# Narrower and longer weight tiles for one q projection, and four gelus written one product later

## The chip, the cores and the metric

The kernel runs on one core of a Trainium2 chip. Time is device microseconds (us) of one execution; a lower number is better. Besides the timed runs there is one profiled execution, whose trace gives start and duration of every instruction on the five engines: PE (TensorE matmuls, with PEld for its weight loads), DVE (VectorE), ACT (ScalarE), POOL (GpSimd) and SP (SyncE, here only the issuing of DMAs).

## The reference

A trunk of two layers over 1024 tokens of width 1024, all in float32. Layer A is a gated MLP whose spatial mixing is per chunk of 128 tokens; layer B is sliding-window attention with sinks; both are wrapped in RMS norms.

```python
# layer A (gmlp_mixer), h = rms_norm(x)
u, v, z = split(h @ w_in, 3)                # 1024 x 2048 each
u = gelu(u)
v = layer_norm(gelu(v), ln_g, ln_b)
s = einsum(causal W_s per chunk and group, v) + b_s
y = (u * s * silu(z)) @ w_out
h1 = x + rms_norm(y)
# shared keys and values
k, v = rms_norm(h1) @ w_k, rms_norm(h1) @ w_v
# layer B (swa_mixer), h = rms_norm(h1)
q, z = split(h @ w_in, 2)                   # 1024 x 1024 each
o = softmax(q k + alibi, with sinks, window 128) v
out = h1 + rms_norm((o * silu(z)) @ w_out)
```

## The kernel before, in words

**Precision.** Each float32 product is made of three fast matmuls: both operands are split into a high part (`hi`, rounded) and a low part (`lo`, what rounding left), and `mm3` (lines 169 to 171) adds hi·hi, hi·lo and lo·hi into one PSUM bank. A split is one ACT instruction for `hi` and one DVE instruction for `lo`: `split` (lines 105 and 106), or `split_scaled` (lines 109 and 110), which multiplies by a gain of one value per partition on the way. The gain belongs to a contraction row block k, so a weight tile that holds several k is split by one `split_scaled` per k.

**Layer A, v.** `v_layer` computes gelu(v) with seven block products instead of eight (a Strassen scheme) for each column half Q. The products come in the order m = 1, 2, 5, 6, 7, 4, 3, each in two steps u = 0, 1 of 24 matmuls. Products 1, 6, 7 and 4 accumulate one after the other in the same four PSUM banks (`vb`); after 1, 6 and 7 ACT copies the running sums out (`copy`, line 209) while the sums stay in the banks, so the next product may write a bank only when its copy is done. Products 2, and 5 with 3, go to four other banks (`vc`). A finished block t gets `done`: a gelu on ACT with the per-token scale `rx` (line 391) and `bn_stats` on DVE (line 392), and the four blocks are stored by one DMA that ACT issues (line 388). For the first block `a1` and for `e67`, the gelus of Q = 0 are written later than their sums, by the table `late` (line 468): `a1` after the matmuls of step (7, 0), `e67` after those of (3, 0). `rx[0]` comes from four token loads, squares on ACT (line 183, tile `junk_x`), a DVE step (line 178) and a power on POOL (line 179). The generator `side` writes these squares, one block of 128 tokens per step from the fifth step on: x_stats(0) in steps (5, 0) to (6, 1), x_stats(1) in steps (7, 0) to (4, 1).

**Layer A, u, z and output projection.** `uz_layer` and `out_layer` follow in the same manner; the first three weight tiles of layer B are loaded towards the end of `out_layer`.

**Layer B.** Tokens go in two halves of 512. For half 0 come q (`q_phase`), the shared k and v (`kv_phase`), then z; half 1 follows, filled in between attention units. `Weights` holds the list of all weight tiles in order, 512 KB each; `wnext` hands out a tile, has the next one split (two `whi`/`wlo` buffers) and the third next loaded (three `raw` buffers, issued by SP). `qz_four` takes four tiles (kq = 0 to 3) for four output blocks m to m+3: a tile holds four m by two k (the 128 x 128 blocks), gives 24 matmuls, and all four banks are complete only in the last of the four tiles. Then `evac` empties each bank: two ACT copies of 64 partitions (line 976, tiles `q_hi` and `q_lo`) and two DVE instructions (line 980). For q of half 0 the first four m use the PSUM banks of tag `mm`, the other four those of tag `s`. `kv_phase` opens four `mm` banks at its start (two `pk`, two `pv`). Beside q of half 0 runs `chain_a(1)`, which finishes layer A's second token half (line 760 on DVE, squares on ACT); beside kv runs `norm_h1(1)`, which transposes on PE into `s` banks (line 776).

**Order.** The order on each engine is not that of the source. The framework's planner walks through the program with its own estimates of durations; whenever an engine is free it is given, of the instructions that the planner then holds to be ready, the one written first. On the chip each engine keeps the order so fixed and waits where an input is late.

Of the kernel before, what the change touches and what calls it, by code (L numbers as in the profile page):

```python
# [19 lines left out]
KT = D // P  # L20
# [7 lines left out]
G_PRE, G_LNG, G_LNB, G_KV, G_BPRE = 0, 8, 24, 40, 48  # L28
# [6 lines left out]
def step(*gens):  # L35
    for g in gens:
        next(g, None)
# [13 lines left out]
def tile_yoco(  # L51
# [29 lines left out]
    def bank(tag, name):  # L81
        return psum.tile([P, 512], F32, tag=tag, name=name)
# [12 lines left out]
    def raw_tile(name):  # L95
        return wpool.tile([P, 1024], F32, tag="raw", name=f"raw_{name}", bufs=3)

    def wload(src, name):
        raw = raw_tile(name)
        dst = raw if len(src.shape) == 2 else raw.rearrange("p (m c) -> p m c", m=4)  # L100
        nc.sync.dma_start(out=dst, in_=src)
        return raw

    def split(hi, lo, src):
        nc.scalar.activation(hi, src, AF.Copy)  # L105
        nc.vector.tensor_tensor(lo, src, hi.bitcast(F32), ALU.subtract)  # L106

    def split_scaled(hi, lo, src, g):
        nc.scalar.activation(hi, src, AF.Copy, scale=g)  # L109
        nc.vector.scalar_tensor_tensor(lo, src, g, hi.bitcast(F32), ALU.mult, ALU.subtract)  # L110

    class Weights:


        def __init__(self):
            self.order = []
            q, z = ([(wqz[i, m:m + 4, :, kq * 256:kq * 256 + 256].rearrange("m p c -> p m c"), f"q{kq}")
                     for m in range(0, 8, 4) for kq in range(4)] for i in range(2))
            kv = [(wkv[kp], f"kv{kp}") for kp in range(4)]
            self.order += q + kv + z + kv + q + z  # L120
            self.order += [(wo_b[gd, cp], "") for gd in range(2) for cp in range(4)]
            self.raw, self.done, self.at = [], [], 0

# [6 lines left out]
        def split(self, i):  # L130
            while len(self.done) <= min(i, len(self.order) - 1):
                n = len(self.done)
                self.load(n)
                raw, kind = self.raw[n], self.order[n][1]
                hi = wpool.tile([P, 1024], F32R, tag="whi", name=f"whi{n}")
                lo = wpool.tile([P, 1024], F32R, tag="wlo", name=f"wlo{n}")
                halves = [slice(kk * 512, kk * 512 + 512) for kk in range(2)]
                if kind[:1] == "q":
                    hv, lv, rv = (t.rearrange("p (m k c) -> p m k c", m=4, k=2) for t in (hi, lo, raw))
                    for k in range(2):  # L140
                        split_scaled(hv[:, :, k], lv[:, :, k], rv[:, :, k], gain(G_BPRE, 2 * int(kind[1:]) + k))
                elif kind[:2] == "kv":
                    for kk, cs in enumerate(halves):
                        split_scaled(hi[:, cs], lo[:, cs], raw[:, cs], gain(G_KV, 2 * int(kind[2:]) + kk))
                else:
                    split(hi, lo, raw)
                self.done.append((hi, lo))
# [10 lines left out]
    def gain(c, k):  # L158
        return gn[:, c + k:c + k + 1]
# [3 lines left out]
    def wnext():  # L163
        w = weights.get()
        weights.ahead()
        return w

    def mm3(out, a_hi, a_lo, b_hi, b_lo, start, stop):
        nc.tensor.matmul(out, lhsT=a_hi, rhs=b_hi, start=start, stop=False, skip_group_check=True)  # L169
        nc.tensor.matmul(out, lhsT=a_hi, rhs=b_lo, start=False, stop=False, skip_group_check=True)  # L170
        nc.tensor.matmul(out, lhsT=a_lo, rhs=b_hi, start=False, stop=stop, skip_group_check=True)  # L171
# [126 lines left out]
    def v_layer(ahead):  # L298
# [140 lines left out]
        a1, e6, e67 = [], None, []  # L439
        for n, (Q, m, u) in enumerate(steps):  # L440
            if u == 0:
                if m == 1:
                    bank_b = [bank("mm", f"vb{Q}_{t}") for t in range(4)]
                elif m in (2, 5):
                    bank_c = [bank("s", f"vc{Q}{m}_{t}") for t in range(4)]
            ps = bank_b if m in (1, 6, 7, 4) else bank_c
            first = m in (1, 2, 5)
            hi, lo = ready.pop(n)
            for kk in range(2):
                k = 2 * u + kk  # L450
                cs = slice(kk * 512, kk * 512 + 512)
                for t in range(4):
                    ts_ = slice(t * P, (t + 1) * P)
                    mm3(ps[t], T[m][0][:, k, ts_], T[m][1][:, k, ts_], hi[:, cs], lo[:, cs],
                        first and k == 0, k == HT - 1)
            if n >= 2:
                prep(n + 2)
            if n >= len(steps) - 3:
                step(ahead)
            if n == 0:  # L460
                xload(xa[:, 1], 0, 1, 0, 2)
            elif n == 1:
                prep(3)
                xload(xa[:, 1], 0, 1, 2, 2)
            elif n >= 4:
                step(side)

            late = {(7, 0): (a1, 0), (3, 0): (e67, 1)}.get((m, u)) if Q == 0 else None
            if late:
                for t in range(4):  # L470
                    done(late[0][t], late[0][t], late[1], late[1], t, Q)
                store(slots[late[1]], late[1], late[1], Q)
            if u == 0:
                continue
            for t in range(4):
                if m == 1:
                    a1.append(slots[0][:, t])
                    copy(a1[t], ps[t])
                elif m == 2:
                    add(a1[t], a1[t], ps[t], ALU.add)  # L480
                    if Q:
                        done(a1[t], a1[t], 0, 0, t, Q)
                elif m == 6:
                    if t == 0:
                        e6 = big.tile([P, 4, TH], F32, tag="P1_3", name=f"ve6_{Q}")
                    copy(e6[:, t], ps[t])
                elif m == 7:
                    e67.append(slots[1][:, t])
                    copy(e67[t], ps[t])
                    add(e67[t], e67[t], bank_c[t], ALU.add)  # L490
                    if Q:
                        done(e67[t], e67[t], 1, 1, t, Q)
                elif m == 4:
                    c = slots[Q][:, t]
                    done(c, ps[t], 1, 0, t, Q)
                elif m == 3:
                    add(e6[:, t], e6[:, t], ps[t], ALU.add)
                    done(e6[:, t], e6[:, t], 0, 1, t, Q)
            block = {3: (e6, 0, 1), 4: (slots[Q], 1, 0)}.get(m)
            if Q and m in (2, 7):  # L500
                block = (slots[0], 0, 0) if m == 2 else (slots[1], 1, 1)
            if block:
                store(*block, Q)
            if m == 3:
                a1, e67 = [], []
            if Q == 1 and m == 2:
                broadcast_rstd(vp)
# [437 lines left out]
    kh = [bp.tile([P, 2, S], F32R, name=f"kh{i}") for i in range(2)]  # L945
# [11 lines left out]

    def qz_four(h, which, m, n, evac):

        tag = "s" if (h, which, m) in ((0, 0, 4), (0, 1, 0)) else "mm"  # L960
        ps = [bank(tag, f"qz{h}_{which}_{m + i}") for i in range(4)]
        for kq in range(4):
            hi, lo = (t.rearrange("p (m k c) -> p m k c", m=4, k=2) for t in wnext())
            for i in range(4):
                for kk in range(2):
                    k = 2 * kq + kk
                    mm3(ps[i], hi[:, i, kk], lo[:, i, kk], n[0][:, k], n[1][:, k], k == 0, k == KT - 1)
                if kq == 3:
                    evac(m + i, ps[i])
                yield  # L970

    def q_phase(h, n, q):
        def evac(m, ps):
            for par in range(2):
                rw = half[par]
                nc.scalar.activation(q[par][rw, m], ps[rw], AF.Copy, scale=qsc[rw, m // 4:m // 4 + 1])
            for par in range(2):
                rw, ot = half[par], half[1 - par]
                g = qsc[rw, m // 4:m // 4 + 1]
                nc.vector.scalar_tensor_tensor(q[par][ot, m], ps[rw], g, q[par][rw, m].bitcast(F32),  # L980
                                               ALU.mult, ALU.subtract)

        for m in range(0, 8, 4):
            yield from qz_four(h, 0, m, n, evac)

    def z_phase(h, n, z, m0, m1):
        def evac(m, ps):
# [314 lines left out]
```

## Time and profile before

| what | value |
|---|---|
| median of three runs | 1050.24 us (1049.72 to 1050.43) |
| the profiled execution's own time | 1051.19 us |
| its span, first to last instruction | 1049.4 us |
| mean granted TensorE clock | 0.998 |
| PE busy | 1038.2 us, 99% of the span |
| DVE, ACT, POOL busy | 731.8, 579.8, 199.5 us |

The span is what the trace covers; the profiled execution's own time holds 1.8 us more, and the median of the unprofiled runs lies 0.95 us below it. A row of the timeline gives start, duration, engine, line, operation, output and inputs with shapes, how often, and in brackets how long the engine sat idle before and who ended that wait. Matmuls overlap: a 128x512 matmul is shown with 0.39 us, but such matmuls start 0.227 us apart.

### The profile page before, as it was taken

How to read it: one execution, taken by the hardware profiler on the slowest of the kernel's cores; microseconds unless marked ns; L12 is line 12 of the kernel's file. 1: busy time of each engine (PE TensorE's matmuls, PEld its weight loads, DVE VectorE, ACT ScalarE, POOL GpSimd, SP SyncE). 2: the span in 40 equal slices, each digit the busy share in tenths (PEclk: the TensorE clock that was granted, in tenths of full speed). 3: DMA queues.
4: the chain of work that ended last, by engine and by line, in shares of the span. 5: the costliest groups of instructions: out<-in, count | busy, mean ns of one | idle time of the engine just before them, and what ended most of it. 6: DMA issues, size and time to landing. Idle time of an engine off the chain costs nothing.

```text
span 1049.4 us, 13678 instructions
## 1 busy us (share of the span) xinstructions
PE 1038.2 (99%) x4994; PEld 854.8 (81%) x4994; DVE 731.8 (70%) x1244; ACT 579.8 (55%) x998; POOL 199.5 (19%) x153
## 2 busy tenths in 40 slices
PE   9999999999999999999999999999999999999997
PEld 7878888888888888888888888888888777877776
DVE  6987566867768668677696587765247786667763
ACT  6584344565565465655444465654466665786631
POOL 0500003253442552530200000100001111011120
PEclk9999999999999999999999999999999999999999
DMA  8878242324333333247998543532322121211363
GB/s 309 271 262 292 101 171 94 116 101 146 126 117 120 123 134 116 101 140 265 320 354 282 195 167 93 200 102 82 99 81 66 56 81 61 81 61 62 121 220 121
DMA packets 80899, 157.56 MB, mean 150 GB/s; under 512 B 5824, under 2 KB 32704, under 8 KB 80832
## 3 DMA queue, kind: packets, MB, share of 16 engines
q1 hardware_dynamic: 76320, 148.01, 41.4%
q10 hardware_dynamic: 4512, 8.68, 2.3%
q8 instruction: 39, 0.64, 0.3%
q14 instruction: 28, 0.23, 0.1%
HBM read 125.21 MB, written 31.46 MB: 149 GB/s over the span
## 4 chain that ended last, share of the span: by engine, by line
PE 93%; DVE 3%; DMA 2%; ACT 1%; issue 0%; SPq 0%; DVEq 0%; POOLq 0%; ACTq 0%
PE qz L169 6%; PE ob L169 6%; PE ub L169 6%; PE qz L171 6%; PE ub L170 6%; PE ub L171 6%; PE ob L171 6%; PE ob L170 6%; PE qz L170 6%; PE s L1058 3%; PE uc L170 3%; PE uc L169 3%; PE uc L171 3%; PE sp L621 3%; PE oc L169 2%; PE oc L171 2%
## 5 line engine op out<-in xcount | busy, mean ns | idle before, releaser
L110 DVE SCALAR_TENSOR_TENSOR wlo<-raw_w,gn,whi 128x512 fp32r<-128x512 f32 x80 | 58.5, 757 | 62.2 <-ACT whi L109 62.0
L169 PE MATMUL qz<-n_hi,whi 128*128 128x512 f32 x256 | 100.9, 394 | 0.0
L171 PE MATMUL qz<-n_hi,wlo 128*128 128x512 f32 x256 | 99.8, 390 | 1.1 <-DVE wlo L110 1.1
L170 PE MATMUL qz<-n_lo,whi 128*128 128x512 f32 x256 | 99.9, 390 | 0.0
L109 ACT ACTIVATE whi<-raw_w,gn 128x512 fp32r<-128x512 f32 x80 | 54.8, 716 | 56.8 <-PE qz L170 36.6
L1073 ACT ACTIVATE pr<-pr,mx 128x129 f32<-128x129 f32 x128 | 50.1, 393 | 39.8 <-DVE mx L1069 39.8
L169 PEld LDWEIGHTS qz<-n_hi,whi 128*128 128x128 f32 x256 | 48.1, 188 | 15.8 <-issue 5.7
L105 ACT ACTIVATE uzhilo_g<-f 128x1024 fp32r<-128x1024 f32 x31 | 32.9, 1060 | 49.2 <-PE uc L171 43.3
L171 PEld LDWEIGHTS qz<-n_hi,wlo 128*128 128x128 f32 x256 | 48.0, 188 | 11.8 <-DVE wlo L110 1.5
L170 PEld LDWEIGHTS qz<-n_lo,whi 128*128 128x128 f32 x256 | 48.1, 188 | 9.3
L106 DVE TENSOR_TENSOR uzhilo_g<-f,uzhilo_g 128x1024 fp32r<-128x1024 f32 x31 | 38.6, 1245 | 19.9 <-ACT uzhilo_g L105 19.9
L209 ACT ACTIVATE uz_slots<-ub 128x512 f32<-128x512 f32 x48 | 28.3, 590 | 42.4 <-PE ub L171 39.2
L169 PE MATMUL ub<-T,whi_g 128*128 128x512 f32 x128 | 50.7, 396 | 0.0
L169 PE MATMUL ub<-T,uzhilo_g 128*128 128x512 f32 x128 | 50.5, 395 | 0.0
L171 PE MATMUL ub<-T,wlo_g 128*128 128x512 f32 x128 | 49.9, 390 | 0.0
L171 PE MATMUL ub<-T,uzhilo_g 128*128 128x512 f32 x128 | 49.9, 390 | 0.0
L170 PE MATMUL ub<-T,uzhilo_g 128*128 128x512 f32 x128 | 49.9, 390 | 0.0
L170 PE MATMUL ub<-T,whi_g 128*128 128x512 f32 x128 | 49.8, 389 | 0.0
L169 PE MATMUL uc<-T,uzhilo_g 128*128 128x512 f32 x124 | 48.9, 395 | 0.0
L170 PE MATMUL uc<-T,uzhilo_g 128*128 128x512 f32 x124 | 48.3, 389 | 0.0
L171 PE MATMUL uc<-T,uzhilo_g 128*128 128x512 f32 x124 | 48.3, 389 | 0.0
L105 ACT ACTIVATE whi_g<-raw_uz 128x1024 fp32r<-128x1024 f32 (+1 forms) x31 | 26.5, 854 | 36.8 <-PE ua L170 14.3
(334 smaller groups left out, 3078.3 us busy)
## 6 DMA issues: line engine op xcount, KB each, us to landing
raw_uz<-in_wuz_in_dram SPq DMA_DIRECT2D x32, 512.0 KB, 3.4
raw_w<-in_wqz_dram SPq DMA_DIRECT2D x32, 512.0 KB, 3.5
td<-uz_slots SPq DMA_DIRECT2D x56, 256.0 KB, 2.2
orawP2a<-td SPq DMA_DIRECT2D x28, 512.0 KB, 4.1
raw<-in_wv_in_dram SPq DMA_DIRECT2D x17, 512.0 KB, 4.8
vg<-vd SPq DMA_DIRECT2D x8, 1024.0 KB, 5.3
orawP2b<-in_wo_a_dram SPq DMA_DIRECT2D x16, 512.0 KB, 8.2
vraw<-in_wv_in_dram SPq DMA_DIRECT2D x13, 512.0 KB, 4.8
```

The lines of the kernel that those rows point to most:

```text
L105: nc.scalar.activation(hi, src, AF.Copy)
L106: nc.vector.tensor_tensor(lo, src, hi.bitcast(F32), ALU.subtract)
L109: nc.scalar.activation(hi, src, AF.Copy, scale=g)
L110: nc.vector.scalar_tensor_tensor(lo, src, g, hi.bitcast(F32), ALU.mult, ALU.subtract)
L169: nc.tensor.matmul(out, lhsT=a_hi, rhs=b_hi, start=start, stop=False, skip_group_check=True)
L170: nc.tensor.matmul(out, lhsT=a_hi, rhs=b_lo, start=False, stop=False, skip_group_check=True)
L171: nc.tensor.matmul(out, lhsT=a_lo, rhs=b_hi, start=False, stop=stop, skip_group_check=True)
L209: nc.scalar.activation(out, a, AF.Copy)
L621: nc.tensor.matmul(psv[:, n], lhsT=d["vg"][:, 4 * j + n, i * P:(i + 1) * P], rhs=d["wc"], start=True, stop=True)
L1058: nc.tensor.matmul(pss[par][:, g, w0:256], lhsT=q[par][:, m, bs_], rhs=w[par][:, p, ks], start=g + k == 0, stop=g + k == 2, skip_group_che ...
L1073: nc.scalar.activation(pr[:, i], pr[:, i], AF.Exp, bias=mx[:, i:i + 1], scale=-1.0, accum_out=dn[:, i:i + 1])
```

## The change

Two edits. First, the weights of q for token half 0 are cut into tiles of two m by four k instead of four m by two k: eight tiles of 512 KB as before, fetched in runs of 512 floats instead of 256. `q_pair` takes two tiles for two output blocks, in two banks, and empties them in the second tile; it uses the `mm` banks throughout. A tile is split by four pairs of ACT and DVE instructions of 128x256 instead of two pairs of 128x512. The number of matmuls, and what they multiply, stays the same; q of half 1 is as before. Second, the four gelus of `a1`, their statistics and their store are written after the matmuls of step (4, 0) instead of (7, 0).

```diff
-        dst = raw if len(src.shape) == 2 else raw.rearrange("p (m c) -> p m c", m=4)
+        dst = raw if len(src.shape) == 2 else raw.rearrange("p (m c) -> p m c", m=src.shape[1])
...
+            qp = [(wqz[0, m:m + 2, :, kh * 512:kh * 512 + 512].rearrange("m p c -> p m c"), f"p{kh}")
+                  for m in range(0, 8, 2) for kh in range(2)]
             kv = [(wkv[kp], f"kv{kp}") for kp in range(4)]
-            self.order += q + kv + z + kv + q + z
+            self.order += qp + kv + z + kv + q + z
...
-                if kind[:1] == "q":
-                    hv, lv, rv = (t.rearrange("p (m k c) -> p m k c", m=4, k=2) for t in (hi, lo, raw))
-                    for k in range(2):
-                        split_scaled(hv[:, :, k], lv[:, :, k], rv[:, :, k], gain(G_BPRE, 2 * int(kind[1:]) + k))
+                if kind[:1] in ("q", "p"):
+                    nk = 2 if kind[0] == "q" else 4
+                    hv, lv, rv = (t.rearrange("p (m k c) -> p m k c", m=8 // nk, k=nk) for t in (hi, lo, raw))
+                    for k in range(nk):
+                        split_scaled(hv[:, :, k], lv[:, :, k], rv[:, :, k], gain(G_BPRE, nk * int(kind[1:]) + k))
...
-            late = {(7, 0): (a1, 0), (3, 0): (e67, 1)}.get((m, u)) if Q == 0 else None
+            late = {(4, 0): (a1, 0), (3, 0): (e67, 1)}.get((m, u)) if Q == 0 else None
...
-        tag = "s" if (h, which, m) in ((0, 0, 4), (0, 1, 0)) else "mm"
+        tag = "s" if (h, which, m) == (0, 1, 0) else "mm"
...
+    def q_pair(m, n, evac):
+
+        ps = [bank("mm", f"qz0_0_{m + i}") for i in range(2)]
+        for kq in range(2):
+            hi, lo = (t.rearrange("p (m k c) -> p m k c", m=2, k=4) for t in wnext())
+            for i in range(2):
+                for kk in range(4):
+                    k = 4 * kq + kk
+                    mm3(ps[i], hi[:, i, kk], lo[:, i, kk], n[0][:, k], n[1][:, k], k == 0, k == KT - 1)
+                    if kk == 1:
+                        yield
+                if kq == 1:
+                    evac(m + i, ps[i])
+                yield
...
-        for m in range(0, 8, 4):
-            yield from qz_four(h, 0, m, n, evac)
+        if h == 0:
+            for m in range(0, 8, 2):
+                yield from q_pair(m, n, evac)
+        else:
+            for m in range(0, 8, 4):
+                yield from qz_four(h, 0, m, n, evac)
```

## The prediction

> **What bounds the kernel now.** I read the page's busy times first, then the table of waits for PE, then busy times by stretch around the two waits that the change aims at, then the timelines there.
>
> ```profile
> PE 1038.2 (99%) x4994; PEld 854.8 (81%) x4994; DVE 731.8 (70%) x1244; ACT 579.8 (55%) x998; POOL 199.5 (19%) x153
> ```
>
> ```profile
> PE vb L169 <- ACT ve L209: 1.3, 1, 1.3
> PE warm L931 <- DVE small L93: 1.1, 1, 1.1
> PE qz L171 <- DVE wlo L110: 1.1, 1, 1.1
> PE vb L169 <- ACT whi_v L105: 0.4, 1, 0.4
> PE vb L169 <- ACT vhi L105: 0.3, 1, 0.3
> PE vb L169 <- ACT T L421: 0.3, 1, 0.3
> ```
>
> PE is busy 99% of the span, and the change leaves its matmuls as they are, so all that can be won is PE's waiting. These six rows are all of its waits; after the warm-up only two exceed 0.4 us: one on an ACT copy (`ve`, line 209) in layer A, one on a weight split (`wlo`, line 110) in layer B's q. Each is one event. The stretches below show what each costs; the first is step (7, 0) of v, the second step (7, 1); then come tiles 1, 2, 3 and 5 of q, half 0, counted from 0.
>
> ```profile
> core 0: us, PE busy (x) PEld busy (x) DVE busy (x) ACT busy (x) POOL busy (x), PEclk, DMA share, GB/s
> 50.84:57.88 7.04, 5.75 (x25) 4.43 (x24) 5.03 (x7) 4.93 (x9) 2.20 (x2) 1.00 0.36 102
> 57.88:63.32 5.44, 5.44 (x25) 4.50 (x24) 5.44 (x7) 5.44 (x9) 0.00 (x0) 1.00 0.95 373
> 660.04:665.48 5.44, 5.44 (x26) 4.51 (x24) 3.90 (x4) 3.53 (x7) 0.14 (x1) 1.00 0.80 287
> 665.48:670.92 5.44, 5.44 (x26) 4.51 (x24) 3.72 (x4) 2.37 (x4) 0.00 (x0) 1.00 0.99 350
> 670.92:676.36 5.44, 5.44 (x26) 4.51 (x24) 3.04 (x6) 5.11 (x10) 1.01 (x1) 1.00 0.54 216
> 681.80:688.63 6.83, 5.78 (x25) 4.39 (x24) 3.55 (x6) 1.33 (x3) 0.00 (x0) 1.00 0.47 142
> ```
>
> Twenty-four matmuls take 5.44 us undisturbed, at full clock (1.00). Step (7, 0) takes 7.04, so it loses 1.60; q's tile 5 takes 6.83 and loses 1.39. These are larger than the waits because PE restarts slowly. Together 2.99 us is the most the change can bring by these two routes.
>
> **The gelus, one product later.** What happens in step (7, 0):
>
> ```profile
> 45.88 0.33 SPq L237 DMA_DIRECT2D raw_xs<-in_x_dram  x1
> 45.67 0.19 ACT L183 ACTIVATION_READ_ACCUMULATOR junk_x<-raw_xs 128x1 f32 x1
> DMA to landing us min/median/max: 3.6/4.4/5.6
> 49.00 1.96 ACT L209 ACTIVATE ve<-vb 128x512 f32<-128x512 f32 x3 [0.29 <-PE vb L171]
> 50.32 0.27 DVE L178 TENSOR_SCALAR rx<-ssx 128x4 f32<-128x4 f32 x1
> 52.03 1.01 POOL L179 TENSOR_TENSOR rx<-rx,small 128x4 f32<-128x4 f32 x1
> 52.65 0.39 PE L171 MATMUL vb<-vhi,T 128*128 128x512 f32 x1
> 53.07 0.72 ACT L391 ACTIVATE vslot<-vslot,rx 128x512 f32<-128x512 f32 x1 [2.11 <-POOL rx L179]
> 53.70 0.58 ACT L209 ACTIVATE ve<-vb 128x512 f32<-128x512 f32 x1
> 54.33 0.50 PE L169 MATMUL vb<-vhi,T 128*128 128x512 f32 x1 [1.29 <-ACT ve L209]
> 60.85 1.04 ACT L183 ACTIVATE junk_x<-raw_xs 128x1024 bf16<-128x1024 f32 x1
> 69.09 0.68 ACT L279 ACTIVATE dg<-ident,rx 128x128 fp32r<-128x128 f32 x2
> ```
>
> Three copies of product 6 end at 50.96. Then, ahead of the fourth copy, stands the first gelu of `a1`, which needs `rx`. DVE's part of `rx` is done at 50.59, but POOL starts its power only at 52.03, so ACT sits still for 2.11 us, the fourth copy runs at 53.70 and PE, which wanted that bank 0.227 us after 52.65, gets it at 54.33. The gelu is written after the fourth copy and runs before it: the planner took it for ready in the short gap before product 6's last block was complete. That planning looks far ahead: `dg` (line 279) is written behind step (2, 1) of Q = 1, which begins seven steps after 63.32, at 101.4, and runs at 69.09.
>
> So writing the gelus later does not by itself take the first one out of that gap; it does so if something written between the old and the new place is ready to fill it. The candidate is the square of the second block of `x_stats(1)`, which ran at 60.85. Its load was issued at 45.88 and lands after 3.6 to 5.6 us, at 49.5 to 51.5; the gap opens at 50.96. If it goes in, ACT spends about 1.25 us (the square and the 0.19 read of its sum), to 52.2, and the copy's 0.58 gives 52.8, in time for PE at 52.88: gain 1.60. If the gelu stays, gain 0. The copy's lateness cannot grow, since nothing in that gap would be slower than the present wait for POOL. I take 1.60, by the median landing (50.3), with a chance just over one half. The three other gelus and the statistics (3 x 0.72 on ACT) move to a stretch where ACT is also nearly full; the copy's readers have 10 us of room there, and the slot that the gelus of product 4 overwrite waits for a store that then starts some 10 us later, with the next use of those banks four steps after 63.32, at 85.1. I cost this at 0; without that room it would be the 2.2 us of the three gelus.
>
> **The q tiles.** The second wait:
>
> ```profile
> 674.42 1.41 DVE L110 SCALAR_TENSOR_TENSOR wlo<-raw_w,gn,whi 128x512 fp32r<-128x512 f32 x2
> 676.53 0.74 DVE L980 SCALAR_TENSOR_TENSOR q_hi<-qz,qsc,q_hi 64x512 fp32r<-64x512 f32 x1
> 681.87 0.76 DVE L980 SCALAR_TENSOR_TENSOR q_lo<-qz,qsc,q_lo 64x512 fp32r<-64x512 f32 x1
> 682.66 2.74 DVE L110 SCALAR_TENSOR_TENSOR wlo<-raw_w,gn,whi 128x512 fp32r<-128x512 f32 x4
> 683.46 0.50 PE L171 MATMUL qz<-n_hi,wlo 128*128 128x512 f32 x1 [1.05 <-DVE wlo L110]
> ```
>
> Four banks complete in one tile, so DVE gets eight instructions at once, 676.53 to 682.63, and only then tile 5's `wlo`, which PE wants at 682.2. With pairs, two blocks complete per two tiles, so DVE's load from `evac` is four instructions (3.0 us) per 10.9 us, and between two of them there is a whole split. The 6.1 us burst is gone and with it the 1.39.
>
> The price is more and smaller splits. The widths that the trace shows:
>
> ```profile
> 46.71 1.04 ACT L105 ACTIVATE T<-xa 128x1024 fp32r<-128x1024 f32 x1
> 47.66 1.05 ACT L105 ACTIVATE whi<-raw 128x1024 fp32r<-128x1024 f32 x1
> 694.04 1.34 ACT L109 ACTIVATE whi<-raw_w,gn 128x512 fp32r<-128x512 f32 x2 [4.10 <-PE qz L170]
> 48.05 1.22 DVE L106 TENSOR_TENSOR T<-xa,T 128x1024 fp32r<-128x1024 f32 x1
> 49.18 1.21 DVE L106 TENSOR_TENSOR wlo<-raw,whi 128x1024 fp32r<-128x1024 f32 x1
> ```
>
> No row is 256 wide. ACT starts 1024-wide splits 0.95 apart and takes 1.34/2 = 0.67 for 512; the line through both gives 0.53 for 256. DVE: 1.13 and 2.74/4 = 0.685, so 0.46. A tile then costs ACT 4 x 0.53 - 1.34 = 0.78 more and DVE 4 x 0.46 - 1.37 = 0.47 more; the bounds are 0 (half the time for half the width) and 1.34 and 1.37 (no saving). For eight tiles that is 6.2 and 3.8 us, all beside PE's 5.44 us per tile: a split and one `evac` fill ACT for 2.12 + 1.38 and DVE for 1.84 + 1.52. On the path: 0. A late quarter also delays PE less, since PE asks for the next k only every 0.68 us.
>
> [...]
>
> The other price is at the handover to `kv_phase`. It opens four `mm` banks at once; before, the last q blocks were in `s` and `mm` was long empty. Now the second `pv` bank must be that of q's last block.
>
> ```profile
> 699.14 0.69 ACT L976 ACTIVATE q_lo<-qz,qsc 64x512 fp32r<-64x512 f32 x1
> 699.51 0.39 PE L169 MATMUL pk<-n_hi,whi 128*128 128x512 f32 x1
> 701.58 0.28 PE L169 MATMUL pv<-whi,n_hi 128*128 128x256 f32 x1
> 702.30 1.04 PE L776 MATMUL nt<-ident,hb 128*128 128x128 f32 x8
> ```
>
> At the boundary ACT first takes half a split (0.67), then two copies (0.69 each), and DVE's second instruction ends about 0.8 later: 2.9 us after kv's start. PE comes to that bank 701.58 - 699.51 = 2.07 after it. Bounds: a wait of 0.85 and a slow restart like the others' (0.2 to 0.3), 1.1; or 0, if the planner puts ready work (the eight transposes, the next `pk`) ahead. I take 0, because the planner draws PE's order with that same wait in view, and the ready work is longer than the wait. The DMAs are eight of 512 KB as before.
>
> **Sum.** Against the profiled execution's own time: 1051.19 - 1.60 - 1.39 = 1048.20. The runs' median lies 0.95 below that execution, so 1047.25, rounded to 1047.3. What follows both places is PE-bound with waits that hang on PE's own progress, so it moves up whole.
>
> **Rivals.**
> (1) The gelu stays in its gap: the wait of 1.29 is there again, 1050.24 - 1.39 = 1048.85. For it: the planner's state at the gap is untouched by the edit, and the square must already be ready in its estimate. Against: the landing above.
> (2) The edit of q works, but the handover waits: 1.1 back, 1048.4 with the gelu's gain, 1049.95 without. For it: 2.9 against 2.07. Against: ready work.
> (3) The split is still late behind `evac`, and only the gelus gain: 1048.6. Against: 3.4 us of DVE work per 5.44.
> (4) Slower. In tiles 1 to 3 of q the work of `chain_a` is still there. DVE is idle 16.32 - 3.90 - 3.72 - 3.04 = 5.66 us in them; three blocks' `evac` (6 x 0.76) and finer splits (3 x 0.47) bring 5.97 there. Tile 4's `wlo` was done at 675.83 for 676.36, 0.53 ahead. If none of that idle time can be used, because it is waiting for ACT and for loads, tile 4 is 5.97 - 0.53 = 5.4 us late and the time is 1052.7. It decides from 2.99 us of lateness, when over half the idle time is unusable. Against: `evac` comes spread, and PE needs only a quarter of a split to go on. [...]
>
> **How the numbers follow.** Forecast 0.40, (1) 0.27, (2) 0.13, (3) 0.09, (4) 0.11. A measurement can tell 0.2%, 2.1 us: faster means under 1048.1, slower over 1052.3. Forecast and a sliver of (2) are faster: 0.42. Cases (1), (2), (3) fall within: 0.48. Case (4) gives 0.10 slower. The likeliest case alone spans 1046.8 to 1047.9 (0.3 us for the bounds on restarts and for the run-to-run spread). The range for all reaches to (2) without the gelu and a first part of (4): 1046.7 to 1050.6.
>
> **What would show it.** Right: PE's table of waits has neither `ve` nor `wlo`, step (7, 0) and all q tiles take 5.44, ACT has a square between the third and fourth `ve`, and DVE never has more than four `evac` instructions in a row. The gelu step is wrong if a `vslot` gelu with `rx` still stands before the fourth `ve`. The handover is wrong if `pv` waits for `q_lo` on DVE. Case (4) shows as `qz` waiting for `wlo` in tiles 2 to 4. My prediction fails above all if planning later in the program is upset and new waits appear in attention, where none is now.

## The result, and the profile after

| | before | after |
|---|---|---|
| median of six runs each, same chip | 1050.50 us (1049.72 to 1050.94) | 1054.03 us (1052.87 to 1054.13) |
| profiled execution's own time | 1051.19 us | 1054.13 us |
| its span | 1049.4 us | 1052.4 us |

The ratio after to before is 1.0031, 95% interval 1.0021 to 1.0041: slower, by about 3.5 us, where 3 us less were forecast. The time lies outside the predicted range.

PE's table of waits in the changed kernel (engine, tile and line that wait, who ends the wait, us in total, times, longest). From line 145 on the line numbers in the changed kernel are three higher than before, and 18 higher in q's evacuation.

```profile
PE vb L172 <- ACT ve L212: 2.6, 1, 2.6
PE warm L934 <- DVE small L93: 1.1, 1, 1.1
PE qz L174 <- DVE wlo L110: 0.8, 1, 0.8
PE vb L172 <- ACT whi_v L105: 0.5, 1, 0.5
PE vb L172 <- ACT vhi L105: 0.3, 1, 0.3
PE pv L172 <- DVE q_lo L998: 0.2, 1, 0.2
```

The wait that the gelu edit was to remove (1.3 before) has doubled. The one that the tiles were to remove went from 1.1 to 0.8, and a small new one stands at the handover to kv. What the first costs is in the busy times by stretch: step (7, 0) of v, then three parts of it.

```profile
core 0: us, PE busy (x) PEld busy (x) DVE busy (x) ACT busy (x) POOL busy (x), PEclk, DMA share, GB/s
50.84:60.78 9.94, 7.33 (x26) 5.60 (x24) 6.53 (x8) 6.24 (x10) 3.51 (x2) 0.83 0.37 120
56.30:57.50 1.20, 1.20 (x5) 0.94 (x4) 0.93 (x1) 1.20 (x3) 0.00 (x0) 0.54 0.00 0
57.50:58.70 1.20, 1.20 (x5) 0.92 (x4) 1.20 (x2) 1.20 (x3) 0.00 (x0) 0.50 0.00 0
58.70:60.00 1.30, 1.30 (x5) 1.05 (x4) 1.30 (x3) 1.30 (x2) 0.00 (x0) 0.58 0.93 224
```

The step takes 9.94 us where it took 7.04, 2.90 more. PE restarts 1.31 us later than before (55.64 against 54.33, row below), and then, from about 56.4 until shortly before 60, it runs at half clock (granted 0.50): the other 1.59. Everything behind comes later by that much, so these 2.9 us are nearly the whole of the span's 3.0. The timelines of that step in the changed kernel, by engine:

```profile
50.31 0.27 DVE L181 TENSOR_SCALAR rx<-ssx 128x4 f32<-128x4 f32 x1
50.49 2.73 DVE L359 SCALAR_TENSOR_TENSOR tch<-xb,gn,tch 128x512 f32<-128x512 f32 x4
...
50.51 2.85 POOL L596 TENSOR_SCALAR_AFFINE_SELECT wc<-wc 128x128 f32<-128x128 f32 x1
53.34 1.01 POOL L182 TENSOR_TENSOR rx<-rx,small 128x4 f32<-128x4 f32 x1
...
54.39 0.72 ACT L394 ACTIVATE vslot<-vslot,rx 128x512 f32<-128x512 f32 x1 [3.43 <-POOL rx L182]
55.01 0.58 ACT L212 ACTIVATE ve<-vb 128x512 f32<-128x512 f32 x1
...
55.64 0.50 PE L172 MATMUL vb<-vhi,T 128*128 128x512 f32 x1 [2.60 <-ACT ve L212]
```

Against them, the same place in the kernel before: three rows of its timelines, then the summary of its eight selects of this kind (min/median/max in ns).

```profile
50.49 1.40 DVE L356 SCALAR_TENSOR_TENSOR tch<-xb,gn,tch 128x512 f32<-128x512 f32 x2
53.83 0.69 DVE L392 BATCH_NORM_STATS2 bst<-vslot 128x6 f32<-128x512 f32 x1 [1.93 <-ACT vslot L391]
50.52 1.53 POOL L593 TENSOR_SCALAR_AFFINE_SELECT wc<-wc 128x128 f32<-128x128 f32 x1
```

```profile
L593 POOL TENSOR_SCALAR_AFFINE_SELECT wc<-wc x8: 294/297/11536, 39.0 to 412.4; 128x128 f32<-128x128 f32 x8
```

The first gelu still stands ahead of the fourth copy. It waits longer for POOL's power, because the select ahead of the power in POOL's queue takes 2.85 us instead of 1.53, where eight selects have a median of 0.30. In both kernels the select ends right after VectorE's run of `tch` subtractions (at 52.05 after 51.89, and at 53.36 after 53.22). That run has four instructions instead of two: before, the first of the gelus' statistics stood behind the first pair in VectorE's order and waited for the gelu (53.83); now the statistics are written one product later, and the planner hands VectorE the second pair at once.

### The profile page after: what moved, and what is told of

It reads as the page before. It is cut to its first block, busy times and chain, and to the rows that moved or that the text cites. A ratio compares the mean times of both kernels' runs of the same rounds, so it can differ in the third digit from the quotient of the medians.

```text
span 1052.4 us, 13708 instructions
## 1 busy us (share of the span) xinstructions
PE 1040.1 (99%) x4994; PEld 856.0 (81%) x4994; DVE 735.0 (70%) x1260; ACT 583.9 (55%) x1014; POOL 200.4 (19%) x153
## 4 chain that ended last, share of the span: by engine, by line
PE 92%; DMA 2%; DVE 2%; POOL 1%; ACT 1%; issue 0%; SPq 0%; DVEq 0%; POOLq 0%; ACTq 0%
PE ob L172 6%; PE ub L172 6%; PE ub L174 6%; PE ub L173 6%; PE ob L173 6%; PE ob L174 6%; PE qz L172 5%; PE qz L174 5%; PE qz L173 5%; PE s L1080 3%; PE uc L173 3%; PE uc L172 3%; PE uc L174 3%; PE sp L624 3%; PE vb L172 2%; PE oc L172 2%
## 5 line engine op out<-in xcount | busy, mean ns | idle before, releaser
L110 DVE SCALAR_TENSOR_TENSOR wlo<-raw_w,gn,whi 128x512 fp32r<-128x512 f32 (+1 forms) x96 | 61.0, 667 | 57.3 <-ACT whi L109 56.8
L109 ACT ACTIVATE whi<-raw_w,gn 128x512 fp32r<-128x512 f32 (+1 forms) x96 | 58.1, 644 | 53.4 <-PE qz L173 32.5
L172 PE MATMUL ub<-T,uzhilo_g 128*128 128x512 f32 x128 | 50.5, 395 | 0.0
```

## The experiments

Ratios are to the kernel before, run on the same chip beside each.

**1. Which edit.** One edit alone, each on the kernel before: the weight tiles, or the one line

```diff
-            late = {(7, 0): (a1, 0), (3, 0): (e67, 1)}.get((m, u)) if Q == 0 else None
+            late = {(4, 0): (a1, 0), (3, 0): (e67, 1)}.get((m, u)) if Q == 0 else None
```

> Only the q tiles are changed; the gelus stay written at step (7, 0). Theory A (the loss of the whole change lies in step (7, 0), where the gelu still stands ahead of the fourth copy and POOL's second select took 2.85 us instead of 1.53; the q edit is worth about nothing: q took 44.59 us instead of 44.91 and the handover gives that back): 1050.5 if POOL's lateness belongs to the gelu edit or to chance, with step (7, 0) at 7.0 us; 1053.5 with step (7, 0) near 9.9 us if the lateness comes with the tile edit. Theory B (the tiles themselves cost the time, by splits late behind evac): 1053 to 1054 with step (7, 0) at 7.0 us.

> Only the gelus are written later; q is as before. The first gelu still stands ahead of the fourth copy in the planned order. Theory A: 1053.5 if POOL's lateness comes with this edit (step (7, 0) near 9.9 us), 1050.5 if it is chance or belongs to the tiles. Theory B: 1050.5, step (7, 0) at 7.0 us.

The tiles alone: 1051.39 us beside 1051.01, ratio 1.0005 (0.9995 to 1.0015), no difference. The gelus alone: 1053.09, ratio 1.0021 (1.0012 to 1.0030), with the second select at 2.85 us and PE's wait at 2.6 again. So the loss comes with the gelu line. In this profiled execution the clock stayed up behind the wait (the step's other matmuls start 0.23 us apart from 56.15 on, where the changed kernel's start 0.43 apart at half clock); PE's restart in the timeline:

```profile
55.81 0.50 PE L169 MATMUL vb<-vhi,T 128*128 128x512 f32 x1 [2.61 <-ACT ve L209]
```

and its span is 1050.9, 1.5 above before and 1.5 below the changed kernel's: close to the two parts of the loss, seen apart, though in one execution of each kernel.

**2. POOL's lateness alone.** Kernel before, with four more selects between its first two:

```diff
             nc.gpsimd.affine_select(wc, wc, [[1, P]], ALU.is_ge, 0.0, base=0, channel_multiplier=-1)
+            if g == 0:
+                scr = const.tile([P, P], F32, name="scr")
+                for _ in range(4):
+                    nc.gpsimd.affine_select(scr, wc, [[1, P]], ALU.is_ge, 0.0, base=0, channel_multiplier=-1)
```

> The kernel before with four more selects of 128x128 on POOL (about 0.3 us each), queued between the first and second select, so that rx comes about 1.2 us later and nothing else is moved. Theory A with the clock (a wait of PE beyond some 2 us is followed by some 3 us at about half clock): wait 2.5 us, granted clock near 0.5 in parts of the step, step (7, 0) 9.5 to 10 us, time 1053.3. Without a clock effect of the wait: step (7, 0) 8.3 us, time 1051.7. If the extra time of the second select was only a wait for something else that the extra selects fill: 1050.5.

1053.76 us, ratio 1.0022 (1.0012 to 1.0032); the power runs at 53.58, PE waits 2.7 and the half clock follows (matmuls 0.43 us apart from 57.23 to 60.22). No gelu was moved: the lateness of POOL's power by itself costs most of what the change costs, or all of it (the intervals overlap).

**3. The gelu out of the gap.** Changed kernel, the gelus of `a1` ordered behind the fourth copy:

```diff
-                for t in range(4):
-                    done(late[0][t], late[0][t], late[1], late[1], t, Q)
+                with tc.issue_after(last6):
+                    for t in range(4):
+                        done(late[0][t], late[0][t], late[1], late[1], t, Q)
```

> The changed kernel with one ordering edge: the four gelus of a1 are issued on ACT behind the fourth copy of product 6. Theory A: PE has no wait for that copy, step (7, 0) is 5.44 us, no half clock, and the time falls by the 4.50 us that the step lost, from 1054.0 to 1049.5. Theory B: step (7, 0) is mended but the time stays above 1052.

A miss: 1053.51 us, ratio 1.0019 (1.0009 to 1.0029). The planner filled the gap with the next thing it held to be ready, which needs `rx` too (ACT's timeline):

```profile
54.54 0.40 ACT L282 ACTIVATE dg<-ident,rx 128x128 fp32r<-128x128 f32 x1 [3.47 <-POOL rx L182]
54.84 0.58 ACT L490 ACTIVATE ve<-vb 128x512 f32<-128x512 f32 x1
```

An instruction in the gap that needs `rx` as the gelu does costs nearly the same (PE waits 2.3 us). A gap filled with one that doesn't need it was not run.

**4. Why the select is long: code loading, a busy VectorE, or VectorE's two inputs.** Four kernels. First, an extra select much earlier, to take any first-use cost (changed kernel):

```diff
+        scr = const.tile([P, P], F32, name="scr")
+        nc.gpsimd.tensor_copy(scr, p0[0][:, 512:640])
+        nc.gpsimd.affine_select(scr, scr, [[1, P]], ALU.is_ge, 0.0, base=0, channel_multiplier=-1)
```

> The kernel after, with one more cast and one more select on POOL right behind the two first casts, at about 8 us, on a scratch tile. Theory L (the first select is long because POOL loads its code then): the added select takes the 11 us, the first of the two real ones 0.3 to 1.5 us from 39.0, both are done by 41, the power ends at about 51.6, the wait for the fourth copy is gone and the time is 1049.3 to 1049.8. Theory H: the added select is short or is held only by VectorE's run there; the first real select still lasts from 39 until VectorE's first pause at about 50.5, the second to 53.3, the wait stays at 2.6 and the time is 1052.5 to 1054.

1053.78 us, ratio 1.0023 (1.0014 to 1.0032). POOL's timeline:

```profile
9.01 0.29 POOL L432 TENSOR_SCALAR_AFFINE_SELECT scr<-scr 128x128 f32<-128x128 f32 x1
39.30 14.14 POOL L599 TENSOR_SCALAR_AFFINE_SELECT wc<-wc 128x128 f32<-128x128 f32 x2 [30.00 <-DMA wc<-in_ws_t_dram]
```

The added first select takes 0.29 us, the two real ones still 14.14 together. So the long times are no first-use cost. Second, only the statistics moved, the gelus left where they were (kernel before):

```diff
-                    done(late[0][t], late[0][t], late[1], late[1], t, Q)
+                    if m == 7:
+                        gelu(late[0][t], late[0][t], 0, t)
+                    else:
+                        done(late[0][t], late[0][t], late[1], late[1], t, Q)
+            if Q == 0 and (m, u) == (4, 0):
+                for t in range(4):
+                    nc.vector.bn_stats(stats[:, t, 0], a1[t])
```

> The kernel before, with nothing changed but that the four statistics instructions of v's first block are written one product later; the gelus stay where they were. The planner then gives VectorE four of tch's subtractions in a row (two before) right behind the root's first step. Theory H (POOL's second select is held as long as VectorE runs instructions with two SBUF inputs without a pause): the select takes 2.85 us instead of 1.53, the power ends at 54.3 to 54.6, TensorE waits 2.6 us for the fourth copy instead of 1.3, and the time is 1052.5 to 1054, that of the changed kernel, although no gelu has moved. Rival G (the gelus' place is the cause, by what ScalarE does): nothing moves, 1050.5 within 0.5. Rival L (the selects' long times are POOL's own, a load of its code): select 1.5 and wait 1.3 as before.

1053.69 us, ratio 1.0021 (1.0011 to 1.0030): the loss without a moved gelu, and VectorE's `tch` run is of four. Not every execution shows it: of ten, seven took 1053.5 or more, two 1050.1 and 1050.7, one 1052.2. The profiled one took 1050.67; in it VectorE happened to wait 0.62 us at 47.55 and the first select ended at 47.70, not at 50.5, so that the second, whose load came at 51.24, was over in 0.58. The long wait behind moved statistics alone is thus shown by the times, not by a trace. Third, the same, with two statistics instructions of 0.69 us (one SBUF input, result unused) between the pairs of `tch`, so that VectorE stays as busy:

```diff
+                if u == 0:
+                    scrd = st.tile([P, 6], F32, name="scrd", bufs=1)
+                    for _ in range(2):
+                        dummy["i"] = nc.vector.bn_stats(scrd, tch[:, 1]).ins
```

> As the run beside it, but behind the second of tch's subtractions VectorE runs two added statistics instructions (one SBUF input each, 0.69 us apiece, the result is used by nothing), so that VectorE is busy as long as in the run beside it, but only the first 1.4 us with instructions of two SBUF inputs. Theory H: the second select ends at about 52.0 again (1.53 us), the power at 53.1, TensorE waits 1.3, and the time is 1050 to 1051. Rival B (any busy VectorE holds POOL): the select takes 2.8, the wait is 2.6 and the time 1052.5 to 1054. Rival L: select 1.5 here and in the run beside it.

VectorE's and POOL's timelines:

```profile
50.50 1.40 DVE L357 SCALAR_TENSOR_TENSOR tch<-xb,gn,tch 128x512 f32<-128x512 f32 x2
51.94 1.43 DVE L361 BATCH_NORM_STATS2 scrd<-tch 128x6 f32<-128x512 f32 x2
...
50.62 1.43 POOL L610 TENSOR_SCALAR_AFFINE_SELECT wc<-wc 128x128 f32<-128x128 f32 x1
52.03 1.01 POOL L179 TENSOR_TENSOR rx<-rx,small 128x4 f32<-128x4 f32 x1
```

VectorE is busy to 53.37, but the select ends at 52.05, when the two-input instructions end, and PE's wait is 1.0. So what held the select here were the `tch` subtractions, VectorE's instructions with two SBUF inputs (they end at 51.90); a busy VectorE as such did not. (VectorE pauses 0.04 us before the added statistics, 51.90 to 51.94; that such a pause isn't needed is seen in the last kernel of this experiment.) The time, 1056.6, missed what was expected for a reason of its own; experiment 6 settles it. Fourth, the selects behind both powers, in the changed kernel and in the kernel before:

```diff
+    pows = {}
...
-        nc.gpsimd.tensor_tensor(dst, dst, nhalf[:, :n], ALU.pow)
+        pows[name] = nc.gpsimd.tensor_tensor(dst, dst, nhalf[:, :n], ALU.pow).ins
...
-            nc.gpsimd.affine_select(wc, wc, [[1, P]], ALU.is_ge, 0.0, base=0, channel_multiplier=-1)
+            with tc.issue_after(pows['x1']):
+                nc.gpsimd.affine_select(wc, wc, [[1, P]], ALU.is_ge, 0.0, base=0, channel_multiplier=-1)
```

> The kernel after, with POOL's two selects put behind the second power of the statistics (nothing needs them so early); the power of the first four is then POOL's first instruction there. Theory H: the power reads SBUF too, so that it is held by tch's run itself: if it starts in the short gap behind the 4-wide step on VectorE it ends by 51.7 and the wait is below 0.5 us, otherwise it ends at about 53.5 to 54.4 and the wait stays at 1.7 to 2.6; time 1049.3 to 1050.2 in the first case, 1052 to 1054 in the second. Theory L (the first select's 11.5 us are a load of POOL's code): the load goes before the power, which starts early enough, and the wait is gone (1049.5), or the load falls into the power and the wait grows to 5 us or more. Theory Q (the selects are only ahead in POOL's queue): the power ends 1.0 us behind its input, at 51.6, and the time is 1049.3.

> The kernel before, with POOL's two selects put behind the second power of the statistics, and nothing else. If TensorE's wait for the fourth copy comes from the selects that stand ahead of the power in POOL's queue, the power ends at about 52.0, the wait falls from 1.3 to 0.2 us and the time is 1.1 us shorter: 1049.4 to 1049.8 beside 1050.6 for before (ratio 0.999). Rival: what is saved there is given back at the next late place, as in the run of the changed kernel with the selects last, where a weight load waited 0.5 us for ScalarE's copy at product 4: 1050.0. Second rival: the selects, now behind, hold up a later stage: 1050.6 or more, with a new wait named in the trace.

Changed kernel: 1050.71 us, ratio 1.0001 (0.9991 to 1.0010): the loss is gone, and PE's wait for the copy is 0.2 us. The time still lies above what each theory gave for a short wait (1050.2 at most); experiment 5 shows what is left. Kernel before: 1049.80, ratio 0.9993 (0.9984 to 1.0002), at the edge of what was expected; the interval just reaches 1. Of the latter, the summary of its selects, then VectorE and POOL at the first two, the power, and PE's restart in the timelines:

```profile
L596 POOL TENSOR_SCALAR_AFFINE_SELECT wc<-wc x8: 288/292/295, 74.7 to 411.3; 128x128 f32<-128x128 f32 x8
```

```profile
74.27 0.69 DVE L394 BATCH_NORM_STATS2 bst<-vslot 128x6 f32<-128x512 f32 x1
74.67 0.54 POOL L596 TENSOR_SCALAR_AFFINE_SELECT wc<-wc 128x128 f32<-128x128 f32 x2
...
50.47 1.44 POOL L181 TENSOR_TENSOR rx<-rx,small 128x4 f32<-128x4 f32 x1 [42.53 <-DVE rx L180]
...
53.21 0.50 PE L169 MATMUL vb<-vhi,T 128*128 128x512 f32 x1 [0.25 <-ACT ve L211]
```

All eight selects take 0.29 us; none is 11.5 us long any more. The first of them runs from its start to its end (74.67 to 74.96) beside one statistics instruction of VectorE, without a pause. PE restarts 1.12 us earlier than before (53.21 against 54.33).

**5. What each edit is worth once POOL's queue is free.** With the selects last: the gelus' line alone; both edits with q's banks emptied one weight tile later; and that kernel with the gelus put back. The later evacuation is

```diff
                 if kq == 1:
-                    evac(m + i, ps[i])
+                    held.append((m + i, ps[i]))
                 yield
+            if kq == 0 or m == 6:
+                while held:
+                    evac(*held.pop(0))
```

> The gelus alone one product later (no new weight tiles), and POOL's two selects behind the second power: what the gelus' edit is worth when the jam on POOL is out of the way. If the edit costs something of its own (the 0.5 us wait for ScalarE's copy at product 4, which the run with both edits showed), the time is 0.4 to 0.5 us above the kernel before with the selects last: 1049.9 to 1050.3. If the edit had the gain that it was priced at, 1.6 us less the 1.1 that the selects already give, it is 0.5 us below that run: 1048.9 to 1049.3. If the loss of the edit had nothing to do with POOL: 1053 as for the gelus alone.

> The changed kernel with the selects last, and in it q's columns are moved out of PSUM one weight tile later (each pair's two after the next pair's first tile). Theory D (the 0.8 us wait in the third weight tile is there because the first pair's four instructions of 0.75 us on VectorE, and the norm's two of 1.28, stand ahead of the split's low parts): the third tile's low parts come earlier, the wait of 0.8 falls below 0.3, the time is 1050.0 to 1050.4 beside 1050.7 for that kernel. Rival: the wait turns up one or two weight tiles later, of the same size, and the time stays at 1050.7. Rival E (the wait is set by ScalarE's high parts, not by VectorE): wait 0.8 at the same place.

> The run before with its gelus of v's first block put back where the kernel before has them: the new weight tiles, the selects last and the later evacuation of q stay. If the gelus' edit costs 0.5 to 0.7 us of its own (the wait for ScalarE's copy at product 4), as the pair of runs without the new tiles has it, the time is 1048.9 to 1049.2 beside 1049.6 for the same kernel with the edit and 1050.6 for the kernel before. Rival: with the new tiles the places of the waits differ, and nothing changes: 1049.6.

The gelus alone: 1050.54 us, ratio 0.9998 (0.9989 to 1.0007), 0.74 above the kernel before with the selects last and above all that was expected but the 1053. A new wait stands at product 4 (PE's timeline):

```profile
62.77 0.50 PE L169 MATMUL vb<-whi,T 128*128 128x512 f32 x1 [0.28 <-ACT vslot L211]
```

Here ACT's copy of product 7 comes only at 62.13, behind a square, where it ran at 60.77 without the edit. So the edit looks like a small loss in itself; the intervals of the two ratios overlap. Both edits with the later evacuation: 1049.61, ratio 0.9991 (0.9982 to 1.0000); the profiled span is 1048.1 against 1049.1 of the changed kernel with the selects last, which differs only in that, and the wait for `wlo` is gone from PE's table (the expectation's third tile is tile 3 when counted from 0). With the gelus put back: 1049.28, ratio 0.9987 (0.9978 to 0.9996), a gain of 1.35 us over the kernel before: the best median of all, and one whose interval leaves out 1. PE's waits in it:

```profile
PE warm L937 <- DVE small L93: 1.1, 1, 1.1
PE vb L172 <- ACT ve L214: 0.5, 1, 0.5
PE vb L172 <- ACT vhi L105: 0.3, 1, 0.3
PE pv L172 <- DVE q_lo L1006: 0.2, 1, 0.2
```

No `qz` row is left. That the gelus cost 0.3 here and 0.7 without the tiles is a difference that these intervals can't tell.

**6. The control that came out 6 us slow.** In the third kernel of experiment 4 no wait grew, yet its time was 1056.6. The scratch tile was made 128 bytes wide instead of 24; then the kernel before got only that tile of 24 bytes and a memset of it:

```diff
+                if u == 0:
+                    scrd = st.tile([P, 6], F32, name="scrd", bufs=1)
+                    nc.vector.memset(scrd, 0.0)
```

> The run with two added statistics instructions again, but the scratch tile that they write has 128 bytes for each partition instead of 24. In that run TensorE's matmuls stood 0.230 to 0.235 us apart instead of 0.227 from 85 to 484 us, with no wait. Theory A (the 24 bytes moved every tile laid out behind it off an even address, and TensorE reads those more slowly): here the matmuls are 0.227 us apart everywhere, the second select ends at about 52.0 with VectorE busy until 53.3, the wait for the fourth copy is 1.0 to 1.3, and the time is 1050 to 1051. Rival: the slow matmuls had to do with that chip at that time or with the added instructions: 1056 again if it is the instructions.

> The kernel before with the scratch tile of 24 bytes for each partition that the added statistics instructions wrote, in the same pool, and one memset of it in their place; nothing else of VectorE's work there changes. Theory A (the tiles laid out behind it are moved, and TensorE reads them more slowly): matmuls 0.230 us apart or more from 85 to 484 us, time 1055 to 1057. Rival (the added statistics instructions, or the order that they bring): 0.227 us apart, 1050.6.

With the wider tile 1055.69 us, ratio 1.0048 (1.0033 to 1.0062): the wait is 1.1, as theory H has it, but the time is still 5 us long, so a rounder size mends little. With the tile alone 1056.75, ratio 1.0056 (1.0041 to 1.0071). So the tile in the layout is the cause, not the added statistics, and beside it the control of experiment 4 (1056.6) has lost nothing to its moved statistics. PE's groups from 85 to 484 us (busy us and mean ns of one matmul), first of the kernel before, then with the scratch tile:

```profile
L169 PE MATMUL ub<-T,whi_g 128*128 128x512 f32 x124 | 49.1, 396 | 0.0
L170 PE MATMUL ub<-T,uzhilo_g 128*128 128x512 f32 x124 | 48.3, 390 | 0.0
```

```profile
L169 PE MATMUL ub<-T,whi_g 128*128 128x512 f32 x124 | 49.1, 396 | 0.0
L170 PE MATMUL ub<-T,uzhilo_g 128*128 128x512 f32 x120 | 47.5, 396 | 0.0
```

Matmuls that read `whi_g` are as before; those that read `uzhilo_g` take 5 to 6 ns more each. With the same tile in the third kernel of experiment 4, the fewer that read v's `vhi` and `vlo` start 0.234 us apart (51.06 to 52.93) instead of 0.227. What exactly about the new addresses does it was not tried.

## Why the prediction was wrong, step by step

**The gelus: the step that failed.** "The copy's lateness cannot grow, since nothing in that gap would be slower than the present wait for POOL." The 1.60 was not won because the square did not go into the gap: the gelu stayed there, which was rival (1), given 0.27. But I priced that rival at no change of this wait, because I took the end of POOL's power, 53.04, as fixed. It wasn't: it hung on a select that took 1.53 us where its like take 0.30, and that select hung on VectorE's run of two-input instructions, which the moved statistics lengthened from two to four. The edit was counted on ACT only; its `bn_stats` on VectorE got the cost 0 with the rest, and what the planner would put in their place was not asked. Rival (4) gave a slower kernel 0.10, but by q's splits, and the tiles alone cost nothing. The sign could have been read from the profile before: an instruction five times as long as its like, right ahead of the critical one, with VectorE's run ending just as it does.

Experiment 4 shows what the select waited for: it took 2.85 us beside four `tch` subtractions, 1.43 beside two and two statistics. It waited out all four, and in the first select's case everything from 39.0 to 50.5, two-input instructions of 1024 columns without a pause. Whether it is the two inputs that hold it, or something else in which these instructions differ from the statistics, no run sets apart. It is not so everywhere: in layer B of the kernel before, POOL does get in between two such instructions.

```profile
1000.04 3.30 DVE L106 TENSOR_TENSOR wob_lo<-raw_ob,wob_hi 128x1024 fp32r<-128x1024 f32 x2 [0.26 <-ACT wob_hi L105]
1000.31 1.96 POOL L1091 TENSOR_SCALAR_AFFINE_SELECT pc<-pc 128x1024 f32<-128x1024 f32 x1
```

This wider select has a median of 1.09 us over its 16. Here it ends at 1002.27, in the midst of the two subtractions, which take 3.30 together where about 2.35 would be usual (1.22 for one, started 1.13 after the other): it seems to have waited for the first, and the second for it. What sets the two cases apart is open.

**The half clock** was in no rival. It adds 1.59 us to a wait of 2.60 (granted clock 0.50 from 56.4 to 59.8), and it came in three of the five profiled executions with waits of 2.3 to 2.7 us (the changed kernel, experiment 2 and the extra early select), and not after the gelus alone (2.61) or the reordered gelus (2.3). Behind the wait of 1.29 in the kernel before, the clock stayed at 1.00. Why one execution has it and another with the same wait has not is not shown.

**The q tiles: the burst went, the gain was mis-sized.** The burst of eight is gone and tile 5 waits no more. But the term of 1.39 came out as 44.91 - 44.59 = 0.32 us over the whole phase, and even that is not clear:

```profile
654.60:699.51 44.91, 43.86 (x193) 35.93 (x192) 28.30 (x41) 24.83 (x42) 3.82 (x3) 1.00 0.48 166
```

```profile
657.47:702.06 44.59, 43.83 (x193) 35.96 (x192) 31.72 (x55) 27.61 (x55) 3.98 (x3) 1.00 0.48 168
```

(q's stretch in the kernel before, then in the changed one). The wait that I meant to remove is no fixed cost. In the profiles of the eight other kernels that have the old tiles, with q's code untouched, PE waits 0.3 to 0.8 us for `wlo` instead of 1.1; in the five with the new tiles and the evacuation unmoved it waits 0.8 to 1.0 (q takes 44.59 us in the changed kernel and 44.57 with the tiles alone). So 1.39 was one high sample, and the tiles by themselves won nothing, as experiment 1 has it. With the new tiles the wait stands in tile 3, counted from 0. VectorE's, ACT's and PE's timelines in the changed kernel:

```profile
670.71 0.48 DVE L110 SCALAR_TENSOR_TENSOR wlo<-raw_w,gn,whi 128x256 fp32r<-128x256 f32 x1
671.11 1.28 DVE L763 SCALAR_TENSOR_TENSOR yoa<-yoa,rpa,xa 128x1024 f32<-128x1024 f32 x1
672.42 0.74 DVE L998 SCALAR_TENSOR_TENSOR q_hi<-qz,qsc,q_hi 64x512 fp32r<-64x512 f32 x1
673.20 1.29 DVE L763 SCALAR_TENSOR_TENSOR yoa<-yoa,rpa,xa 128x1024 f32<-128x1024 f32 x1
674.51 0.76 DVE L998 SCALAR_TENSOR_TENSOR q_lo<-qz,qsc,q_lo 64x512 fp32r<-64x512 f32 x1
675.30 0.88 DVE L110 SCALAR_TENSOR_TENSOR wlo<-raw_w,gn,whi 128x256 fp32r<-128x256 f32 x2
...
686.26 1.68 DVE L110 SCALAR_TENSOR_TENSOR wlo<-raw_w,gn,whi 128x256 fp32r<-128x256 f32 x4 [1.21 <-ACT whi L109]
...
685.72 1.71 ACT L109 ACTIVATE whi<-raw_w,gn 128x256 fp32r<-128x256 f32 x4 [2.19 <-PE qz L173]
...
675.84 0.50 PE L174 MATMUL qz<-n_hi,wlo 128*128 128x512 f32 x1 [0.76 <-DVE wlo L110]
705.86 0.36 PE L172 MATMUL pv<-whi,n_hi 128*128 128x256 f32 x1 [0.23 <-DVE q_lo L998]
```

Between two parts of tile 3's split VectorE runs two `chain_a` steps and two instructions of the evacuation, 4.2 us (671.11 to 675.30). Rival (4) named just this, `chain_a` and evacuation together in the early tiles, but priced it at 5.4 us and at tile 4; it was 0.76 at tile 3. Against rival (3) I set "3.4 us of DVE work per 5.44" and left out that `chain_a` counts in the same tiles. In experiment 5 only the evacuation was moved; the wait was gone, and 1.0 us of span with it. Whether a later evacuation would do as much with the old tiles was not run. The split's prices were too high: four of 256 take 1.71 on ACT and 1.68 on VectorE, against 2.12 and 1.84.

**The handover** was inside its bounds: the planner did put the transposes and two `pk` ahead, and 0.23 us of wait is left of the 0.85. I took 0.

**What bounds the kernel** was right for the kernel before: PE's waits are what can be won. In the changed one part of the loss, 1.59 us, was no wait, but TensorE's clock (0.50). And of "the most", 2.99 us, the best kernel got 1.35, with the gelus left in place and two edits, the selects and the evacuation, that the change did not have.

## What to carry to other kernels

Before an edit that only moves instructions is priced at nothing, look at each engine on which it leaves a hole, and ask what the planner will put there; here the hole was VectorE's and the victim POOL. An instruction that takes several times its like's duration ahead of a critical one may be a wait in disguise: find out what holds it, and move it out of the queue (with two selects put later the changed kernel's ratio to before fell from 1.0031 to 1.0001). A wait is not always paid once only: behind three of the four profiled waits of 2.6 us or more TensorE then ran at half clock, in the changed kernel for 3.4 us. And a wait read from one profile can be a high sample: look for it in other profiles of the same code before its whole length is put into a sum.

## What the runs showed of the hardware that was not expected

- A select of 0.29 us on POOL took 2.85 and 11.5 us, until VectorE's run of two-input instructions paused (53.36 after 53.22) or turned to an instruction with one input (50.55 after 50.31). In layer B a select of 1.09 us seems to have waited for one such instruction only: it took 1.96, and ended in the midst of the next. The power of four columns, a two-input instruction itself, was not held so: beside the four `tch` subtractions, in the changed kernel with the selects last, it took 1.45 us instead of 1.01. Why these differ stays open.
- After an idle time of 2.60 us TensorE ran 3.4 us at half clock (0.50), and of the five profiled executions with idle times of 2.3 to 2.7 us only three show a half clock.
- 24 bytes of scratch in an early pool made the matmuls that read `uzhilo_g` 1.5% longer (396 against 390 ns) and the kernel 6 us slower, with no wait in PE's table above 1.1 us. Kernels that differ in their tiles' places can't be compared to a few us without looking at the matmuls' mean durations.
